# The gate matrix of a PEER layer from 2-byte one-hots made on VectorE, with the gate in three 2-byte parts

## The chip, the core and the metric

The kernel runs on one core of a Trainium2 chip. The metric is the device time in microseconds (us) of one execution. Before the change it is 2056.32 us, the median of three runs (2055.21 to 2059.06).

## The reference, cut to what matters

One layer of a diffusion backbone: a token-mixing part (differential attention, a spatial gating branch, gated merge) and then a channel-mixing part, PEER: 512 tokens, 8 heads, and for each token and head the best 16 of 128 x 128 = 16384 single-neuron experts.

```python
s1, i1 = lax.top_k(s[:, :, 0], 16)       # per token and head, 128 keys on each side
s2, i2 = lax.top_k(s[:, :, 1], 16)
cand = s1[..., :, None] + s2[..., None, :]          # 256 candidates
best, pos = lax.top_k(cand, 16)
eidx = (i1 * 128 + i2) picked by pos                # expert number
gate = softmax(best)
act = gelu(x . u_tab[eidx]) * gate                  # per token, head, pick
out = sum over picks of act * v_tab[eidx]
```

So each token has 128 picks (8 heads x 16), each with a first key number, a second key number and a gate in 4-byte floats.

## The kernel before, in words

The layer runs as one hand-ordered program. The engines POOL, VectorE (DVE), ScalarE (ACT) and TensorE (PE) execute their instructions in the order in which the code emits them (`manual_schedule`, `by_hand`, L218 and L692). The token-mixing part comes first and is not touched.

PEER is done in two ways. One block of 128 tokens (block 3) gathers its picks row by row with indirect DMAs on POOL (`fetch`, `dot`, `accumulate`, L805 to L823, stepped by `gather_to`, L836). The other three blocks (NB = 3, 384 tokens) are computed densely against all 16384 experts, 128 experts at a time: `u_pass(b)` (L773) makes GELU(u . x) for 128 experts and 384 tokens on PE with 24 matmuls, writes it through the SP queue to HBM for the first 74 passes, and `v_pass(b)` (L1156) later multiplies by the gate matrix G and by the second table. Each pass takes its weights from a loader (`w_get`, L192): a DMA on the SP queue, `w_hi` on ACT (L170), `w_lo` on DVE (L181), three passes ahead with three buffers each.

G is what the change is about. For one token, G is a 128 x 128 matrix: entry (first key, second key) is the gate of that pick. The kernel makes it as a matrix product over the 128 picks: a one-hot of the second key of every pick (`oa`, picks on the partitions, 128 keys along the free dimension) times a one-hot of the first key scaled with the gate (`ob`). The stage has 48 batches (t, o) of 8 tokens each.

- `picks_of(t)` (L1035): three PE transposes of a block's key numbers and gates, and one ACT copy to `pk`.
- `one_hots_a` (L1049): ACT, eight Square activations of 128 elements (iota minus key, squared) and one Relu of 1024 elements (1 minus it) per batch.
- `one_hots_b` (L1058): DVE, eight TENSOR_SCALAR of 128 elements per batch (equal to the key, times the gate).
- `gate_matrix` (L1067): PE, eight 4-byte matmuls of 128 x 128 x 128 per batch (the profile has two records for each), two ACT copies out of PSUM into `stg`, and after each second batch one DMA of 1 MB to HBM (`G_d`, L1081).

The loop (L1095 to L1106) emits for batch i: one-hots b of batch i+1, the gate matmuls of batch i, one `u_pass`, one-hots a of batch i+2, some 2.8 us of the top-16 and merge work of later blocks on DVE (`advance`, L946, until that is used up), the second half of a gather step that is pending (`gather_end`, L825), and from batch 10 to 42 new gather steps: a dot on DVE, a fetch on POOL. A gather step's GELU (L818) is on ACT, between a dot and an `acc` on DVE. After the loop come the last u passes, and then the v passes, of which the first needs a load of G back from HBM (`Gc`, L1142).

Of the kernel before, what the change touches and what calls it, by code (L numbers as in the profile page):

```python
# [13 lines left out]
F32 = mybir.dt.float32  # L14
F32R = mybir.dt.float32r
BF16 = mybir.dt.bfloat16
I32 = mybir.dt.int32
U32 = mybir.dt.uint32
AF = mybir.ActivationFunctionType
ALU = mybir.AluOpType  # L20
# [4 lines left out]
P = 128  # L25
# [33 lines left out]
def body(ctx, nc, tc, a, out):  # L59
# [11 lines left out]
    ones = cp.tile([P, P], F32, name="ones")  # L71
# [284 lines left out]
    with att, tc.tile_pool(name="at1", bufs=1) as a1, tc.tile_pool(name="at2", bufs=2) as a2, \  # L356
# [6 lines left out]
        for k in range(2):  # L363
            nc.vector.scalar_tensor_tensor(ld, lamr[:, k * 128:k * 128 + 64], 1.0, lamr[:, k * 128 + 64:k * 128 + 128],
                                           op0=ALU.mult, op1=ALU.mult, accum_out=le[:, k:k + 1])
# [171 lines left out]
    with tc.tile_pool(name="sg1", bufs=1) as s1, tc.tile_pool(name="sg2", bufs=2) as s2:  # L537
# [6 lines left out]
        with tc.tile_pool(name="pz", bufs=1, space=PSUM) as pzp, tc.tile_pool(name="pu", bufs=2, space=PSUM) as pu:  # L544
# [10 lines left out]
            for half in range(2):  # L555
                pz = [pzp.tile([P, 512], F32, name=f"pz{t}") for t in range(NT)]
                for c2 in range(4):
# [6 lines left out]
                    for cc in range(2):  # L564
                        c = c2 * 2 + cc
                        r = slice(cc * 512, cc * 512 + 512)
                        for t in range(NT):
                            q = slice(t * P, t * P + P)
# [82 lines left out]
            for j in range(NH):  # L651
                po = pu.tile([P, T], F32, name="ps_ot", tag="ps_m")
                for t in range(NT):
# [3 lines left out]
                                               op0=ALU.mult, op1=ALU.subtract)  # L657
# [3 lines left out]
            for i, n in enumerate(LAST):  # L661
# [14 lines left out]
                                           op0=ALU.add, op1=ALU.mult)  # L676
# [16 lines left out]
    with tc.tile_pool(name="o1", bufs=1) as o1, tc.tile_pool(name="o2", bufs=2) as o2:  # L693
        rowt = {}
        for i, k in enumerate(("gg1", "sh2", "gsc2")):
            t = o1.tile([P, D], F32, name=f"row_{k}")
# [128 lines left out]
    def gather_end(left=0):  # L825
        while len(pend) > left:
            accumulate(*pend.pop(0))
# [8 lines left out]
    def gather_to(share):  # L836
        while steps and n_steps - len(steps) < n_steps * share:
            gather_step()

    gS = {}  # L840
    with tc.tile_pool(name="k1", bufs=1, side="right") as k1:
        iota_i = k1.tile([P, P], I32, name="iota_i")
        nc.gpsimd.iota(iota_i, pattern=[[1, P]], base=0, channel_multiplier=0)
        iota = k1.tile([P, P], F32, name="iota")
# [88 lines left out]
        def next_u():  # L933
            if nu[0] < n_ahead:
                gS[nu[0]] = u_pass(nu[0])
                nu[0] += 1
# [9 lines left out]
        def advance(us):  # L946

            while us > 0 and any(todo):
                q = todo[0] or todo[1]
                d = next(q[0], None)  # L950
                if d is None:
                    q.popleft()
                else:
                    us -= d
            return any(todo)
# [73 lines left out]

        with tc.tile_pool(name="pg", bufs=3, space=PSUM) as pgp, tc.tile_pool(name="k2", bufs=2, side="right") as k2:  # L1030
            stg = {}

            pks, oas, obs = {}, {}, {}

            def picks_of(t):  # L1035

                while t not in pks:
                    while t not in done:
                        advance(1.0)
                    ef = efs.pop(t)  # L1040
                    pt = pgp.tile([P, 3, P], F32, name="ps_pk", bufs=1)
                    for k in range(2):
                        nc.tensor.transpose(pt[:, k], ef[:, k].rearrange("p h k -> p (h k)"), ident)
                    nc.tensor.transpose(pt[:, 2], gate[:, t], ident)
                    pks[t] = k2.tile([P, 3, P], F32, name="pk")
                    nc.scalar.activation(pks[t], pt, AF.Copy)
                return pks[t]

            def one_hots_a(t, o):  # L1049

                pk = picks_of(t)
                oa = oas[t, o] = k2.tile([P, 8, P], F32, name="oh_a", bufs=3)
                for i in range(8):
                    k = o * 8 + i
                    nc.scalar.activation(oa[:, i], iota, AF.Square, scale=-1.0, bias=pk[:, 1, k:k + 1])  # L1055
                nc.scalar.activation(oa, oa, AF.Relu, scale=-1.0, bias=ones[:, 0:1])

            def one_hots_b(t, o):  # L1058

                t0 = o * 8  # L1060
                pk = picks_of(t)
                ob = obs[t, o] = k2.tile([P, 8, P], F32, name="oh_b")
                for i in range(8):
                    nc.vector.tensor_scalar(ob[:, i], iota, pk[:, 0, t0 + i:t0 + i + 1], pk[:, 2, t0 + i:t0 + i + 1],  # L1064
                                            op0=ALU.is_equal, op1=ALU.mult)

            def gate_matrix(t, o):  # L1067

                oa, ob = oas.pop((t, o)), obs.pop((t, o))
                if o % 2 == 0:  # L1070
                    stg[0] = k2.tile([P, NBLK // GCH, 16, GCH], F32, name="stg")
                for q in range(2):
                    pG = pgp.tile([P, 4, P], F32, name="ps_G")
                    for i in range(4):
                        nc.tensor.matmul(pG[:, i], oa[:, q * 4 + i], ob[:, q * 4 + i], start=True, stop=True)  # L1075
                    tt = o % 2 * 8 + q * 4
                    nc.scalar.activation(stg[0][:, :, tt:tt + 4].rearrange("p c t g -> p t c g"),
                                         pG.rearrange("p t (c g) -> p t c g", g=GCH), AF.Copy)
                if o % 2:
                    tt = t * P + o // 2 * 16  # L1080
                    nc.sync.dma_start(G_d[:, :, tt:tt + 16].rearrange("c p t g -> p c (t g)"),  # L1081
                                      stg[0].rearrange("p c t g -> p c (t g)"))

            batches = [(t, o) for t in range(NB) for o in range(16)]
            while 0 not in done:
                advance(4.0)
                next_u()
            for _ in range(UA):
                next_u()
            one_hots_a(*batches[0])  # L1090
            for _ in range(UB):
                next_u()
            one_hots_a(*batches[1])
            one_hots_b(*batches[0])
            for i, (t, o) in enumerate(batches):  # L1095
                if i + 1 < len(batches):
                    one_hots_b(*batches[i + 1])
                gate_matrix(t, o)
                if nu[0] < n_ahead - RESERVE:
                    next_u()  # L1100
                if i + 2 < len(batches):
                    one_hots_a(*batches[i + 2])
                advance(2.8)
                gather_end()
                if i >= G_FROM:
                    gather_to(PICKS_G * (i + 1 - G_FROM) / (G_TO - G_FROM) if i < G_TO else 0)  # L1106
            advance(1000.0)
            while nu[0] < n_ahead:
                next_u()
# [181 lines left out]
```

## Time and profile before

| | before |
|---|---|
| median of 3 runs, us | 2056.32 |
| the profiled execution, us | 2059.31 |
| its span (first to last instruction), us | 2057.1 |
| mean granted TensorE clock | 0.984 |
| stage of the gate matrix: first gate matmul to the start of the last batch's, us in the span | 955.1 to 1271.5 |

The profiled execution's own time is 3 us above the median; differences are worked out against it and then put onto the median. "Idle before, releaser" in a row is the time that the engine stood still before the instruction and what ended that. In a timeline row, "xN" means N instructions of the same kind one after the other, and the duration is that of all of them. PEld is the weight load of a matmul, which overlaps with PE. A wait for several things is put down to the one that came last.

### The profile page before, as it was taken

How to read it: one execution, taken by the hardware profiler on the slowest of the kernel's cores; microseconds unless marked ns; L12 is line 12 of the kernel's file. 1: busy time of each engine (PE TensorE's matmuls, PEld its weight loads, DVE VectorE, ACT ScalarE, POOL GpSimd, SP SyncE). 2: the span in 40 equal slices, each digit the busy share in tenths (PEclk: the TensorE clock that was granted, in tenths of full speed). 3: DMA queues.
4: the chain of work that ended last, by engine and by line, in shares of the span. 5: the costliest groups of instructions: out<-in, count | busy, mean ns of one | idle time of the engine just before them, and what ended most of it. 6: DMA issues, size and time to landing. Idle time of an engine off the chain costs nothing.

```text
span 2057.1 us, 28286 instructions
## 1 busy us (share of the span) xinstructions
PE 1928.1 (94%) x10042; PEld 1693.9 (82%) x10042; DVE 1609.0 (78%) x3070; ACT 1016.5 (49%) x1963; POOL 451.5 (22%) x275
## 2 busy tenths in 40 slices
PE   5699999999999899889899999899999999999997
PEld 3478888887888788688888999688888889999996
DVE  6957777736766657999998785688888789899987
ACT  4345555544333355446989987333333333333333
POOL 4832232101000124330002110011111233333321
PEclk9899999999999999999999999999999999999999
DMA  7452323344867355346659999899998789989982
GB/s 240 162 158 71 98 72 98 88 159 136 263 210 239 123 163 162 117 160 214 188 183 318 309 316 295 306 322 334 324 334 317 270 340 353 342 326 344 348 313 98
DMA packets 167772, 473.91 MB, mean 230 GB/s; under 512 B 14000, under 2 KB 82512, under 8 KB 149072
## 3 DMA queue, kind: packets, MB, share of 16 engines
q1 hardware_dynamic: 149200, 337.89, 49.4%
q0 software_dynamic: 18432, 134.23, 17.8%
q8 instruction: 79, 1.29, 0.2%
q14 instruction: 61, 0.50, 0.1%
HBM read 415.29 MB, written 48.38 MB: 225 GB/s over the span
## 4 chain that ended last, share of the span: by engine, by line
PE 63%; DVE 19%; issue 7%; DMA 5%; ACT 4%; POOL 1%; SPq 0%; ACTq 0%; DVEq 0%; POOLq 0%
PE po L200 8%; PE po L201 8%; PE po L199 8%; PE ps_u L201 5%; PE ps_u L200 5%; PE ps_u L199 5%; DVE w_lo L181 3%; PE ps_G L1075 2%; PE ps_proj L199 2%; PE ps_proj L200 2%; PE ps_proj L201 2%; DVE ada_j L274 2%; PE ps_s L455 2%; DMA ada_w<-in_wada 2%; ACT oh_a L1055 1%
## 5 line engine op out<-in xcount | busy, mean ns | idle before, releaser
L170 ACT ACTIVATE w_hi<-w_raw 128x1024 fp32r<-128x1024 f32 x370 | 390.8, 1057 | 458.5 <-issue 280.2
L181 DVE TENSOR_TENSOR w_lo<-w_raw,w_hi 128x1024 fp32r<-128x1024 f32 x324 | 397.9, 1229 | 170.7 <-ACT w_hi L170 170.1
L807 POOL DMA_INDIRECT uv<-in_uv,eidx x128 | 207.5, 1621 | 876.1 <-DVE acc L823 536.8
L201 PE MATMUL ps_u<-h2B,w_lo 128*128 128x384 f32 x1024 | 348.3, 340 | 16.4 <-DVE w_lo L181 16.4
L199 PE MATMUL ps_u<-h2B,w_hi 128*128 128x384 f32 x1024 | 352.3, 344 | 1.1 <-ACT h2B L739 1.1
L200 PE MATMUL ps_u<-h2B,w_hi 128*128 128x384 f32 x1024 | 347.0, 339 | 0.6 <-DVE r L84 0.6
L199 PE MATMUL po<-w_hi,ah 128*128 128x512 f32 x768 | 303.8, 396 | 7.5 <-ACT ah L1148 7.5
L200 PE MATMUL po<-w_lo,ah 128*128 128x512 f32 x768 | 303.7, 396 | 0.2 <-DVE w_lo L181 0.2
L201 PE MATMUL po<-w_hi,al 128*128 128x512 f32 x768 | 303.8, 396 | 0.0
L201 PEld LDWEIGHTS ps_u<-h2B,w_lo 128*128 128x128 f32 x1024 | 194.2, 190 | 19.3 <-DVE w_lo L181 19.3
L199 PEld LDWEIGHTS ps_u<-h2B,w_hi 128*128 128x128 f32 x1024 | 194.9, 190 | 4.1 <-ACT h2B L739 1.4
L200 PEld LDWEIGHTS ps_u<-h2B,w_hi 128*128 128x128 f32 x1024 | 194.6, 190 | 3.8 <-DVE r L84 1.0
L199 PEld LDWEIGHTS po<-w_hi,ah 128*128 128x128 f32 x768 | 144.4, 188 | 40.4 <-ACT ah L1148 7.8
L201 PEld LDWEIGHTS po<-w_hi,al 128*128 128x128 f32 x768 | 144.2, 188 | 35.0
L200 PEld LDWEIGHTS po<-w_lo,ah 128*128 128x128 f32 x768 | 144.3, 188 | 33.9 <-DVE w_lo L181 1.0
L823 DVE SCALAR_TENSOR_TENSOR acc<-uv,act,acc 128x1024 f32<-128x1024 f32 x127 | 163.2, 1285 | 4.5
L814 DVE SCALAR_TENSOR_TENSOR dj<-uv,h2A 128x1024 bf16<-128x1024 f32 x128 | 156.2, 1220 | 0.9
L181 POOL TENSOR_TENSOR w_lo<-w_raw,w_hi 128x1024 fp32r<-128x1024 f32 x46 | 114.7, 2497 | 180.0 <-ACT w_hi L170 179.9
L1146 DVE TENSOR_TENSOR at<-gS,Gc 128x384 f32<-128x384 f32 x128 | 120.9, 945 | 8.1 <-DMA gS<-gS_d 8.1
L1148 ACT ACTIVATE ah<-at 128x384 fp32r<-128x384 f32 x128 | 65.9, 515 | 123.6 <-DVE at L1146 123.5
L781 ACT ACTIVATE gS<-ps_u 128x384 f32<-128x384 f32 x128 | 62.7, 490 | 127.9 <-PE ps_u L201 127.3
L1075 PE MATMUL ps_G<-oh_b,oh_a 128*128 128x128 f32 x768 | 100.8, 284 | 24.8 <-DVE oh_b L1064 24.3
(302 smaller groups left out, 3562.6 us busy)
## 6 DMA issues: line engine op xcount, KB each, us to landing
w_raw<-in_uT SPq DMA_DIRECT2D x128, 512.0 KB, 5.8
w_raw<-in_uv SPq DMA_DIRECT2D x128, 512.0 KB, 6.6
w_raw<-in_w SPq DMA_DIRECT2D x120, 512.0 KB, 3.6
G_d<-stg SPq DMA_DIRECT2D x24, 1024.0 KB, 6.0
Gc<-G_d SPq DMA_DIRECT2D x16, 1536.0 KB, 9.9
w_raw<-in_wada SPq DMA_DIRECT2D x32, 512.0 KB, 4.4
gS_d<-gS SPq DMA_DIRECT2D x74, 192.0 KB, 4.0
gS<-gS_d SPq DMA_DIRECT2D x74, 192.0 KB, 4.6
```

Of the source, the lines that this page charges most:

```text
L170: nc.scalar.activation(hi, r, AF.Copy)
L181: eng.tensor_tensor(lo, r, hi.bitcast(F32), op=ALU.subtract)
L199: nc.tensor.matmul(ps, lh, rh, start=first, stop=False)
L200: nc.tensor.matmul(ps, lh, rl, start=False, stop=False)
L201: nc.tensor.matmul(ps, ll, rh, start=False, stop=last)
L781: nc.scalar.activation(g, ps, AF.Gelu)
L807: nc.gpsimd.indirect_dma_start(out=g, out_offset=None, in_=a["uv"], in_offset=bass.IndirectOffsetOnAxis(ap=eidx[:, t - NB, k:k + 1], axis=0))
L814: nc.vector.scalar_tensor_tensor(junk, g[:, :D], 1.0, h2A[t - NB], op0=ALU.mult, op1=ALU.mult, accum_out=act)
L823: nc.vector.scalar_tensor_tensor(acc[t - NB], g[:, D:], act, acc[t - NB], op0=ALU.mult, op1=ALU.add)
L1075: nc.tensor.matmul(pG[:, i], oa[:, q * 4 + i], ob[:, q * 4 + i], start=True, stop=True)
L1146: nc.vector.tensor_tensor(at, gS.pop(b), Gc[b // GCH][:, :, b % GCH], op=ALU.mult)
L1148: nc.scalar.activation(ah, at, AF.Copy)
```

## The change

The one-hots become 2-byte floats (key numbers up to 127 are exact in them), made for eight tokens by one DVE instruction each; ACT makes none any more. A gate of 24 bits is split into three 2-byte parts whose sum is the gate, so `ob` has three tiles, and the gate matmul of one token becomes three matmuls that add up in PSUM. Per batch DVE gets five TENSOR_TENSOR of 1024 elements (`oa`, `eq`, three products) in place of eight TENSOR_SCALAR of 128 elements; ACT loses eight Square and one Relu; PE has 24 matmuls of 2-byte data in place of 16 records of 4-byte data. The per-token operand is stored twice side by side ([P, 5, P, 2]) so that its innermost dimension is a run of two elements. `picks_of` gets two more ACT copies and two DVE subtractions. `oa` has two buffers and not three, and it is made one batch ahead and not two.

```diff
@@ -1029,7 +1029,9 @@
 
         with tc.tile_pool(name="pg", bufs=3, space=PSUM) as pgp, tc.tile_pool(name="k2", bufs=2, side="right") as k2:
             stg = {}
-
+            PAIR = [P, 8, P // 2, 2]
+            iota2 = k2.tile([P, P // 2, 2], BF16, name="iota2", bufs=1)
+            nc.vector.tensor_copy(iota2, iota.rearrange("p (a b) -> p a b", b=2))
             pks, oas, obs = {}, {}, {}
 
             def picks_of(t):
@@ -1042,27 +1044,37 @@
                     for k in range(2):
                         nc.tensor.transpose(pt[:, k], ef[:, k].rearrange("p h k -> p (h k)"), ident)
                     nc.tensor.transpose(pt[:, 2], gate[:, t], ident)
-                    pks[t] = k2.tile([P, 3, P], F32, name="pk")
-                    nc.scalar.activation(pks[t], pt, AF.Copy)
+                    pk = pks[t] = k2.tile([P, 5, P, 2], BF16, name="pk")
+                    nc.scalar.activation(pk[:, 0:3], pt.unsqueeze(3).to_broadcast([P, 3, P, 2]), AF.Copy)
+                    rest_ = k2.tile([P, P], F32, name="g_rest", bufs=1)
+                    nc.vector.tensor_tensor(rest_, pt[:, 2], pk[:, 2, :, 0], op=ALU.subtract)
+                    for k in range(3, 5):
+                        nc.scalar.activation(pk[:, k], rest_.unsqueeze(2).to_broadcast([P, P, 2]), AF.Copy)
+                        if k == 3:
+                            nc.vector.tensor_tensor(rest_, rest_, pk[:, k, :, 0], op=ALU.subtract)
                 return pks[t]
 
+            def per_token(pk, k, o):
+                return pk[:, k, o * 8:o * 8 + 8].unsqueeze(2).to_broadcast(PAIR)
+
+            def pairs(x):
+                return x.rearrange("p t (a b) -> p t a b", b=2)
+
             def one_hots_a(t, o):
 
+                oa = oas[t, o] = k2.tile([P, 8, P], BF16, name="oh_a")
+                nc.vector.tensor_tensor(pairs(oa), iota2.unsqueeze(1).to_broadcast(PAIR), per_token(picks_of(t), 1, o),
+                                        op=ALU.is_equal)
+
+            def one_hots_b(t, o):
+
                 pk = picks_of(t)
-                oa = oas[t, o] = k2.tile([P, 8, P], F32, name="oh_a", bufs=3)
-                for i in range(8):
-                    k = o * 8 + i
-                    nc.scalar.activation(oa[:, i], iota, AF.Square, scale=-1.0, bias=pk[:, 1, k:k + 1])
-                nc.scalar.activation(oa, oa, AF.Relu, scale=-1.0, bias=ones[:, 0:1])
-
-            def one_hots_b(t, o):
-
-                t0 = o * 8
-                pk = picks_of(t)
-                ob = obs[t, o] = k2.tile([P, 8, P], F32, name="oh_b")
-                for i in range(8):
-                    nc.vector.tensor_scalar(ob[:, i], iota, pk[:, 0, t0 + i:t0 + i + 1], pk[:, 2, t0 + i:t0 + i + 1],
-                                            op0=ALU.is_equal, op1=ALU.mult)
+                eq = k2.tile([P, 8, P], BF16, name="oh_e", bufs=1)
+                nc.vector.tensor_tensor(pairs(eq), iota2.unsqueeze(1).to_broadcast(PAIR), per_token(pk, 0, o),
+                                        op=ALU.is_equal)
+                ob = obs[t, o] = k2.tile([P, 3, 8, P], BF16, name="oh_b")
+                for k in range(3):
+                    nc.vector.tensor_tensor(pairs(ob[:, k]), pairs(eq), per_token(pk, 2 + k, o), op=ALU.mult)
 
             def gate_matrix(t, o):
 
@@ -1072,7 +1084,8 @@
                 for q in range(2):
                     pG = pgp.tile([P, 4, P], F32, name="ps_G")
                     for i in range(4):
-                        nc.tensor.matmul(pG[:, i], oa[:, q * 4 + i], ob[:, q * 4 + i], start=True, stop=True)
+                        for k in range(3):
+                            nc.tensor.matmul(pG[:, i], oa[:, q * 4 + i], ob[:, k, q * 4 + i], start=k == 0, stop=k == 2)
                     tt = o % 2 * 8 + q * 4
                     nc.scalar.activation(stg[0][:, :, tt:tt + 4].rearrange("p c t g -> p t c g"),
                                          pG.rearrange("p t (c g) -> p t c g", g=GCH), AF.Copy)
@@ -1088,18 +1101,16 @@
             for _ in range(UA):
                 next_u()
             one_hots_a(*batches[0])
+            one_hots_b(*batches[0])
             for _ in range(UB):
                 next_u()
-            one_hots_a(*batches[1])
-            one_hots_b(*batches[0])
             for i, (t, o) in enumerate(batches):
                 if i + 1 < len(batches):
+                    one_hots_a(*batches[i + 1])
                     one_hots_b(*batches[i + 1])
                 gate_matrix(t, o)
                 if nu[0] < n_ahead - RESERVE:
                     next_u()
-                if i + 2 < len(batches):
-                    one_hots_a(*batches[i + 2])
                 advance(2.8)
                 gather_end()
                 if i >= G_FROM:
```

## Rows read from the trace of the kernel before

**Rows 1.** The page's part 1: engine, busy us, share of the span, instructions

```profile
PE 1928.1 (94%) x10042; PEld 1693.9 (82%) x10042; DVE 1609.0 (78%) x3070; ACT 1016.5 (49%) x1963; POOL 451.5 (22%) x275
```

**Rows 2.** Windows A, B, C: us, busy PE, PEld, DVE, ACT, POOL; PEclk, DMA share, GB/s

```profile
955.14:1067.76 112.62, 102.38 (x643) 98.69 (x644) 108.86 (x331) 99.81 (x214) 0.13 (x1) 0.98 0.57 174
1067.76:1253.60 185.84, 172.19 (x1124) 168.71 (x1124) 148.42 (x347) 166.79 (x387) 33.23 (x23) 1.00 0.94 310
1253.60:1271.50 17.90, 17.90 (x121) 17.90 (x121) 10.04 (x29) 17.53 (x39) 0.00 (x0) 1.00 0.91 285
```

**Rows 3.** Timeline of stretch A, one batch (start us, us, instruction): DVE, then PE

```profile
1044.02 2.14 DVE L1064 TENSOR_SCALAR oh_b<-iota,pk 128x128 f32<-128x128 f32 x8
1046.06 1.22 DVE L181 TENSOR_TENSOR w_lo<-w_raw,w_hi 128x1024 fp32r<-128x1024 f32 x1
1047.20 1.22 DVE L912 TENSOR_TENSOR eq<-ij,iota 128x1024 f32<-128x1024 f32 x1
1048.45 1.22 DVE L916 TENSOR_TENSOR eq<-eq,idxf 128x1024 f32<-128x1024 f32 x1
...
1050.85 2.13 DVE L1064 TENSOR_SCALAR oh_b<-iota,pk 128x128 f32<-128x128 f32 x8
...
1051.34 2.19 PE L1075 MATMUL ps_G<-oh_b,oh_a 128*128 128x128 f32 x16 [0.46 <-DVE oh_b L1064]
```

**Rows 4.** Timeline of stretch B, one batch: ACT, DVE, PE

```profile
1120.95 0.49 ACT L781 ACTIVATE gS<-ps_u 128x384 f32<-128x384 f32 x1 [1.59 <-PE ps_u L201]
1121.34 2.44 ACT L1055 ACTIVATE oh_a<-iota,pk 128x128 f32<-128x128 f32 x8
...
1124.87 0.18 ACT L818 ACTIVATE act<-act 128x1 f32<-128x1 f32 x1
...
1125.09 0.16 DVE L819 TENSOR_TENSOR act<-act,gate 128x1 f32<-128x1 f32 x1 [1.80 <-ACT act L818]
...
1128.12 2.19 PE L1075 MATMUL ps_G<-oh_b,oh_a 128*128 128x128 f32 x16 [1.24 <-DVE oh_b L1064]
```

**Rows 5.** Timeline of stretch C: two gate groups on PE

```profile
1259.57 1.95 PE L1075 MATMUL ps_G<-oh_b,oh_a 128*128 128x128 f32 x16
...
1265.53 1.95 PE L1075 MATMUL ps_G<-oh_b,oh_a 128*128 128x128 f32 x16
```

**Rows 6.** Timeline behind the stage: SP, then PE

```profile
1274.11 0.37 SPq L1081 DMA_DIRECT2D G_d<-stg  x1
...
1293.48 0.79 PE L199 MATMUL po<-w_hi,ah 128*128 128x512 f32 x1 [7.53 <-ACT ah L1148]
```

**Rows 7.** Groups by form, 955 to 1275 us: count, busy us, mean ns, idle before

```profile
L912 DVE TENSOR_TENSOR eq<-ij,iota 128x1024 f32<-128x1024 f32 x8 | 9.8, 1219 | 0.0
...
L821 DVE TENSOR_SCALAR acc<-uv,act 128x1024 f32<-128x1024 f32 x1 | 0.8, 752 | 0.0
L877 DVE TENSOR_TENSOR cand<-val 128x512 f32<-128x512 f32 x1 | 0.7, 693 | 0.0
...
L923 DVE TENSOR_TENSOR gate<-gate,gz 128x128 f32<-128x128 f32 x2 | 0.6, 292 | 0.1
```

**Rows 8.** Timeline of PE: first and last of 7 starts with 384 columns, of 6 with 512

```profile
1262.06 0.34 PE L200 MATMUL ps_u<-h2B,w_hi 128*128 128x384 f32 x1
...
1263.10 0.34 PE L200 MATMUL ps_u<-h2B,w_hi 128*128 128x384 f32 x1
...
1399.85 0.40 PE L199 MATMUL po<-w_hi,ah 128*128 128x512 f32 x1
...
1401.01 0.39 PE L201 MATMUL po<-w_hi,al 128*128 128x512 f32 x1
```

**Rows 9.** Timeline of the stage's first us: ACT, then DVE

```profile
948.38 0.48 ACT L1046 ACTIVATE pk<-ps_pk 128x384 f32<-128x384 f32 x1
...
953.51 1.23 DVE L181 TENSOR_TENSOR w_lo<-w_raw,w_hi 128x1024 fp32r<-128x1024 f32 x1 [2.26 <-ACT w_hi L170]
...
960.27 1.23 DVE L181 TENSOR_TENSOR w_lo<-w_raw,w_hi 128x1024 fp32r<-128x1024 f32 x1 [1.42 <-ACT w_hi L170]
```

## The prediction

> **What bounds the kernel now.** I read the page's part 1 first: PE is busy for 94% of the span, ACT for 49% [rows 1]. That mean says nothing of the stage that is edited, so I cut the stage into three stretches by the starts of the gate groups [rows 2]. A holds batches 0 to 15 (16 in 112.62 us, 7.04 a batch), B batches 16 to 43 (28 in 185.84, 6.64 a batch), C batches 44 to 46 (5.97 a batch). In A the DVE is busy 108.86 of 112.62 us: it is full, with the top-16 and merge work of later blocks beside the one-hots. In B it is busy 148.42 of 185.84 (5.30 a batch), PE 172.19. In C PE has no gap at all.
>
> One batch of A [rows 3]: oh_b starts at 1044.02, w_lo and merge work follow back to back, the next oh_b starts at 1050.85. The gate group on PE starts at 1051.34, after 0.46 us of idle ended by DVE's oh_b, and takes 2.19 us because it follows oh_b token by token. So A goes at DVE's pace, and ACT's speed is of no use there. One batch of B [rows 4]: ACT finishes a u pass with gS at 1120.95, and only after eight Squares and a Relu comes the small act of a gather step, at 1124.87. DVE has waited 1.80 us for it, runs the acc and dot behind it, then oh_b, and PE's next gate group starts 1.24 us late. In B the work that leaves ACT does stand on the path, in some batches. In C PE's own period shows: 1259.57 to 1265.53 is 5.96 us, one gate group and one u pass [rows 5]. Behind the stage the last gate group sets the end: its G goes to HBM at 1274.11, and PE stands 7.53 us idle until the first v pass starts at 1293.48 [rows 6]. The u passes that are left finish inside that gap, so a shift of the last gate group moves the end by as much.
>
> **What DVE loses and gets.** Out go eight TENSOR_SCALARs a batch: 1046.06 - 1044.02 = 2.04 us of DVE [rows 3]. In come five TENSOR_TENSORs of 1,024 2-byte elements. No row shows a TENSOR_TENSOR with all operands of two bytes. From above: 4-byte ones of this size take 1.219 us [rows 7], start to start 1.14 where independent and 1.25 where one reads the other's result [rows 3]. From below: a 128-element oh_b starts every 0.255 us (2.04 / 8), and no DVE instruction with eight times the elements should go under that. Between them, the one-source TENSOR_SCALAR of 1,024 elements takes 0.752, and the 512-element TENSOR_TENSOR 0.693 [rows 7]; 1.219 against 0.693 gives 1.03 ns an element. I take two 2-byte elements in the time of one 4-byte element, the price of the 512-element row: 0.693 - 0.08 (the overlap in 1.22 to 1.14) = 0.61 independent, and 0.72 for the one that waits for eq. A batch is 4 x 0.61 + 0.72 = 3.16, so +1.12 on DVE.
>
> The Trainium skill (Vector Engine (DVE) Microarchitecture Reference, section 5.1) says two-source ops take two 2-byte elements a cycle when every operand's innermost step is one and longer than one element; the doubled operand meets that, and by it the price is mine. Its section 5.2 speaks against: a port that does not read adjacent pairs of 4-byte words from an 8-byte boundary loses about 0.65 cycle an element; worked out from its figures this is an estimate of some 1.0 us an instruction.
>
> A row bears on that: L912 reads one operand's element 16 times in a row and still takes 1.219, like w_lo with dense operands [rows 3, 7]. A repeated read cost nothing there, so the sum keeps 0.61.
>
> **Stretch A and the start.** The one-hots of batches 0 to 16 are made up to A's end: 17 x 1.12 = 19.0 us on a full DVE. Against that, two waits of DVE for w_hi at the start, 2.26 and 1.42 us [rows 9], stand behind the Squares and Relus on ACT and go. Net +15. Cover lost: PE's gate group can no longer follow oh_b token by token, as its first matmul needs the third product. That costs nothing while DVE sets the pace: gate group plus u pass is under 6 us against 8 on DVE.
>
> **The picks, three times.** ACT's pk copy takes 0.48 for 384 elements [rows 9]; with each element stored twice I put 0.8. Then DVE subtracts (0.29, the 128-element row [rows 7]), ACT copies (0.3 to 0.5), DVE subtracts, ACT copies. DVE stands in order: behind the first subtraction wait the one-hots, w_lo and the merge. Some 1 us a block, since oa and eq cover the last copy: +3. On PE the transposes keep their place; the block-1 dot now lies ahead of the subtraction and covers the pk copy. The cast of iota is one 0.3 us instruction. SP's and POOL's queues keep their order.
>
> **PE.** Six starts of 384 columns take 1.04 us, 0.173 each [rows 8]; a u pass has 24, 4.15. The period of 5.96 [rows 5] leaves 1.81 to the gate group's 16 starts, 0.113 each. The new group has 24 starts. Lower end: five starts of 512 columns take 1.16, 0.232 each [rows 8], so 128 columns are 0.059 and 128 columns alone 0.173 - 2 x 0.059 = 0.055; with a little on top I write 0.066, a group of 1.6 and a period of 5.75. Upper end: 0.113 again, a group of 2.7 and a period of 6.87. The 128-column row is slower than its columns, and what is left to explain that is the weight load. With 2-byte weights half as many bytes are loaded, so I take a value under 0.098, where PE (4.15 plus 24 starts) stays under DVE's period in B. The upper end stays for the range and as a rival.
>
> **Stretch B.** DVE's work is 5.30 + 1.12 = 6.42 a batch. The waits for act go: with no Square and Relu between gS and act, act comes about 3.5 us earlier (1121.34 to 1124.87 [rows 4]). 23 of the 28 batches have a gather step (POOL's count [rows 2]); without one DVE works 10.04 / 3 = 3.35 a batch as in C [rows 2], 4.5 after the change, with one some 6.8. The short batches cannot use all they gain, since the next acc still waits for the u pass. I put 6.46 in place of 6.64: 28 x 0.18 = -5. What is late next is DVE itself. The transfers stand near: share 0.94 at 6.64 [rows 2], so no period under 6.64 x 0.94 = 6.24.
>
> **Stretch C.** PE sets the pace: 3 x (5.97 - 5.75) plus the last group, -1.
>
> **Sum:** +15 + 3 - 5 - 1 = +12. The profiled execution, 2059.3, is 3 us over the median; on the median, 2056.3 + 12 = 2068.
>
> **The rivals.**
> 1. *DVE at the full price.* Each TENSOR_TENSOR costs as a 4-byte one: 4 x 1.14 + 1.25 = 5.8 a batch, +3.8. A gets 17 x 3.8 - 4 = +61, B goes to 9.1, 28 x 2.5 = +69, C +3, picks +3: +136, 2192. The 752 ns row shows a DVE that can do better with one source [rows 7], none shows it with two. 0.09.
> 2. *The repeated word is read at less than full pace.* The per-token operand reads the same four bytes 64 times in a row, in all five instructions. Halfway between 0.61 and 1.14, 0.87, a batch is 4 x 0.87 + 0.99 = 4.5, +2.4: A 17 x 2.4 - 4 = +37, B 28 x (7.7 - 6.64) = +30, picks +3: +70, 2126. L912 speaks against it [rows 7]. 0.04. This is the case of the skill's section 5.2, above.
> 3. *PE becomes the bound in B and C.* At 0.113 a start B goes to 6.87, 28 x 0.23 = +6, and C with the last group gets +4: +15 + 3 + 6 + 4 = +28, 2084. For it: the same 128-column shape. Against: half the bytes. 0.20.
> 4. *The other side: the one-hots cost DVE no more than now, and the ACT waits of B go.* Place: the five instructions. It decides where A's loss equals B's gain, which the transfers cap at 28 x 0.40 = 11: 17 x (added) - 4 + 3 - 1 = 11 gives 0.76 added a batch, 0.54 an instruction; under about 0.48 the kernel is faster by over 0.2%. At 0.40 it is 17 x 0.08 - 4 + 3 - 11 - 1 = -12, 2044. Against: 0.54 is no more than 512 elements at the 1.03 ns of the rows. 0.05.
> 5. *B fills up fully.* My price holds, but B reaches its 6.24 and the start hides a little more: +13 + 3 - 11 - 1 = +4, 2060. 0.09.
>
> **How the numbers follow.** My forecast has 0.53. A measurement of this kernel can tell about 0.2%, 4 us, from no change. Slower: forecast, rivals 1 to 3, 0.85; within 0.2%: most of rival 5 and a little of the forecast's spread, 0.10; faster 0.05. The range takes in rivals 5 and 3 with the spread of the picks (2 below the one, 4 above the other), 2058 to 2088; it leaves out rivals 1, 2 and 4, 0.18.
>
> **What would show it.** Right: in A a period near 8 us with DVE without gaps and PE idle about 2 us a batch ahead of the gate group, ended by DVE's ob; 0.69 for a TENSOR_TENSOR; in B ACT idle, no wait of DVE for act over 1 us, periods of 6.3 to 6.6; gate starts under 0.098. Wrong: DVE instructions at 1.2; PE without a gap in B; a granted clock that drops in A, where PE stands longer (it is 0.98 there now [rows 2]), enough that the u passes outlast DVE's 8 us; or gaps on DVE in A that I took for work.

## The result, and the profile after

The changed kernel takes 2068.64 us (median of 5 runs, 2067.29 to 2069.57), the kernel before 2056.87 in the same comparison: a ratio of 1.0054, 95% interval 1.0041 to 1.0067. That is 11.8 us slower; +12 and 2068 were forecast. The number is right, but not every term of it: a wait that was left out (+4.3) and a gain that was put too small (by 4.6) cancel, as the stretches and run 1 show. That the total came out so near is luck in part.

The same three stretches as in [rows 2], cut at the starts of the same gate groups (us, busy PE, PEld, DVE, ACT, POOL; granted clock, DMA share, GB/s), of the changed kernel:

```profile
957.54:1087.99 130.45, 105.85 (x773) 97.77 (x771) 127.07 (x286) 48.67 (x74) 0.94 (x1) 0.92 0.49 149
1087.99:1265.23 177.24, 164.16 (x1347) 153.86 (x1348) 175.00 (x260) 77.33 (x138) 33.73 (x22) 1.00 0.99 327
1265.23:1282.05 16.82, 16.82 (x145) 16.31 (x145) 14.17 (x20) 7.91 (x12) 0.00 (x0) 1.00 1.00 323
```

A went from 112.62 to 130.45 us (+17.8), B from 185.84 to 177.24 (-8.6), C from 17.90 to 16.82 (-1.1). DVE is now full in A and in B (127.07 of 130.45, 175.00 of 177.24), ACT is busy for less than half of either. The stage begins 2.4 us later in its span (957.54 against 955.14), although this execution was 1.0 us ahead shortly before (run 1 has the rows).

The groups by form of the changed kernel over the stage: count, busy us, mean ns, idle before (`oh_e` is the name of the tile `eq`):

```profile
L1077 DVE TENSOR_TENSOR oh_b<-oh_e,pk 128x1024 bf16<-128x1024 bf16 x144 | 90.9, 686 | 1.7
L1088 PE MATMUL ps_G<-oh_b,oh_a 128*128 128x128 bf16 x1145 | 85.5, 223 | 37.7 <-DVE oh_b L1077 37.7
L1088 PEld LDWEIGHTS <-oh_a 128*128 128x128 bf16 x1146 | 69.0, 99 | 56.7 <-issue 32.7 <-DVE oh_b L1077 23.2 <-DVE w_lo L181 0.3
...
L1073 DVE TENSOR_TENSOR oh_e<-iota,pk 128x1024 bf16<-128x1024 bf16 x47 | 32.1, 683 | 0.0
L1066 DVE TENSOR_TENSOR oh_a<-iota,pk 128x1024 bf16<-128x1024 bf16 x47 | 32.1, 683 | 0.0
```

A 1,024-element instruction on 2-byte operands takes 0.683 to 0.686 us, within 0.01 us of the 512-element 4-byte row [rows 7]. The timeline of one batch of A, DVE and then PE, of the changed kernel:

```profile
1058.45 0.68 DVE L1066 TENSOR_TENSOR oh_a<-iota,pk 128x1024 bf16<-128x1024 bf16 x1
1059.05 0.69 DVE L1073 TENSOR_TENSOR oh_e<-iota,pk 128x1024 bf16<-128x1024 bf16 x1
1059.77 1.89 DVE L1077 TENSOR_TENSOR oh_b<-oh_e,pk 128x1024 bf16<-128x1024 bf16 x3
...
1061.58 1.22 DVE L181 TENSOR_TENSOR w_lo<-w_raw,w_hi 128x1024 fp32r<-128x1024 f32 x1
```

```profile
1060.52 0.23 PE L1088 MATMUL ps_G<-oh_b,oh_a 128*128 128x128 bf16 x1 [1.10 <-DVE oh_b L1077]
1061.11 0.22 PE L1088 MATMUL ps_G<-oh_b,oh_a 128*128 128x128 bf16 x1 [0.37 <-DVE oh_b L1077]
1061.71 1.39 PE L1088 MATMUL ps_G<-oh_b,oh_a 128*128 128x128 bf16 x22 [0.38 <-DVE oh_b L1077]
1068.43 0.23 PE L1088 MATMUL ps_G<-oh_b,oh_a 128*128 128x128 bf16 x1 [1.10 <-DVE oh_b L1077]
```

From oh_a to the w_lo behind the products is 3.13 us (1058.45 to 1061.58), where oh_b took 2.04 [rows 3]. This batch lasts 7.91 us (1060.52 to 1068.43) against 6.83 in the same place before. PE waits 1.10 us ahead of the group and twice 0.4 inside it, once for each further product.

What the prediction had at almost nothing is the cast of iota (DVE, changed kernel):

```profile
919.08 0.23 DVE L1034 CAST iota<-iota 128x128 bf16<-128x128 f32 x1 [4.35 <-PE ps_sc L984]
```

The matmuls that end this wait, on PE:

```profile
917.99 1.05 PE L984 MATMUL ps_sc<-keysT,qT 128*128 128x128 f32 x8
```

DVE stands still for 4.35 us. The tile for the 2-byte iota is taken from a pool that opens where the query stage's pool closes, so its memory is that of tiles of which the last is read by the score matmuls L984; those stand behind a u pass on PE.

In B no wait for act is left: over all of B DVE waited 26.7 us for it before the change, in 11 waits, and not once after. The timeline of one batch of B in the changed kernel, ACT and then DVE (compare [rows 4]):

```profile
1107.44 0.19 ACT L818 ACTIVATE act<-act 128x1 f32<-128x1 f32 x1
...
1108.07 1.22 DVE L181 TENSOR_TENSOR w_lo<-w_raw,w_hi 128x1024 fp32r<-128x1024 f32 x1
...
1109.20 0.15 DVE L819 TENSOR_TENSOR act<-act,gate 128x1 f32<-128x1 f32 x1
1109.39 1.28 DVE L823 SCALAR_TENSOR_TENSOR acc<-uv,act,acc 128x1024 f32<-128x1024 f32 x1
```

The act is done 1.6 us before DVE comes to it. Behind the stage nothing changed: from the start of the last gate group to the end of the span it is 785.8 us, 785.6 before, and PE stands there as in [rows 6]:

```profile
1303.62 0.79 PE L199 MATMUL po<-w_hi,ah 128*128 128x512 f32 x1 [7.51 <-ACT ah L1159]
```

### The profile page after: what moved, and what is told of

Read it like the earlier page. It is cut to its first block, busy times and chain, and to the rows that moved or that the text cites. A ratio compares the mean times of both kernels' runs of the same rounds, so it can differ in the third digit from the quotient of the medians.

```text
span 2067.8 us, 28429 instructions
## 1 busy us (share of the span) xinstructions
PE 1926.7 (93%) x10426; PEld 1680.6 (81%) x10426; DVE 1657.6 (80%) x2933; ACT 863.6 (42%) x1537; POOL 457.5 (22%) x275
## 3 DMA queue, kind: packets, MB, share of 16 engines
q0 software_dynamic: 18432, 134.23, 17.6%
## 4 chain that ended last, share of the span: by engine, by line
PE 62%; DVE 25%; issue 7%; DMA 3%; ACT 2%; POOL 1%; SPq 0%; POOLq 0%; DVEq 0%; ACTq 0%
PE po L199 8%; PE po L201 8%; PE po L200 8%; PE ps_u L201 5%; PE ps_u L199 5%; PE ps_u L200 5%; DVE w_lo L181 4%; DVE oh_b L1077 3%; PE ps_proj L199 2%; PE ps_proj L200 2%; PE ps_proj L201 2%; DVE ada_j L274 2%; PE ps_s L455 2%; PE ps_o L489 1%; DMA w_raw<-in_wada 1%
## 5 line engine op out<-in xcount | busy, mean ns | idle before, releaser
L807 POOL DMA_INDIRECT uv<-in_uv,eidx x128 | 212.6, 1661 | 882.7 <-DVE acc L823 551.7
L199 PE MATMUL ps_u<-h2B,w_hi 128*128 128x384 f32 x1024 | 356.7, 348 | 1.1 <-ACT h2B L739 1.1
L200 PE MATMUL ps_u<-h2B,w_hi 128*128 128x384 f32 x1024 | 350.8, 343 | 0.6 <-DVE r L84 0.6
L199 PEld LDWEIGHTS ps_u<-h2B,w_hi 128*128 128x128 f32 x1024 | 197.9, 193 | 4.3 <-ACT h2B L739 1.5
L200 PEld LDWEIGHTS ps_u<-h2B,w_hi 128*128 128x128 f32 x1024 | 197.8, 193 | 3.8 <-DVE r L84 1.0
L814 DVE SCALAR_TENSOR_TENSOR dj<-uv,h2A 128x1024 bf16<-128x1024 f32 x128 | 156.1, 1219 | 0.9
L1088 PE MATMUL ps_G<-oh_b,oh_a 128*128 128x128 bf16 x1152 | 85.9, 223 | 37.7 <-DVE oh_b L1077 37.7
```

The source lines that it names most:

```text
L199: nc.tensor.matmul(ps, lh, rh, start=first, stop=False)
L200: nc.tensor.matmul(ps, lh, rl, start=False, stop=False)
L807: nc.gpsimd.indirect_dma_start(out=g, out_offset=None, in_=a["uv"], in_offset=bass.IndirectOffsetOnAxis(ap=eidx[:, t - NB, k:k + 1], axis=0))
L814: nc.vector.scalar_tensor_tensor(junk, g[:, :D], 1.0, h2A[t - NB], op0=ALU.mult, op1=ALU.mult, accum_out=act)
L1088: nc.tensor.matmul(pG[:, i], oa[:, q * 4 + i], ob[:, k, q * 4 + i], start=k == 0, stop=k == 2)
```

## The experiments

Theory: in A and in B VectorE sets the pace, so a batch's cost is what its one-hots cost DVE; the gain in B is that act no longer stands behind one-hot work on ACT; the cast's wait adds 4 us. Rivals: the 24 matmuls set the pace, or the gain in B comes from ACT's smaller load or the shorter gate groups. Rows of windows below have the columns of [rows 2].

**1. The 2-byte iota made early (iota_early).**

```diff
-            iota2 = k2.tile([P, P // 2, 2], BF16, name="iota2", bufs=1)
+        iota2 = k1.tile([P, P // 2, 2], BF16, name="iota2")   # and its cast, at the start of the PEER part
```

> The changed kernel with the 2-byte iota made at the start of the PEER part, in a buffer of its own, and not in the pool whose memory the query stage held until then. Theory: the cast's wait of 4.35 us on VectorE lies on the full engine ahead of stretch A, so nearly all of it comes back: about 2064.5 us, 4 us under the changed kernel, the three stretches as they were (130, 177, 17 us). Rival: the 3.3 us by which the stage began late in the changed kernel are drift between two executions, or VectorE makes up for them elsewhere: 2068.6 us.

2063.99 us (ratio to before 1.0031, 1.0020 to 1.0043), 4.65 under the changed kernel between the medians. The first gate group starts at 954.60, A and B stay:

```profile
954.60:1085.10 130.50, 106.45 (x772) 98.43 (x770) 127.11 (x286) 48.97 (x74) 0.94 (x1) 0.91 0.49 149
1085.10:1262.44 177.34, 164.22 (x1347) 153.84 (x1348) 175.10 (x260) 77.35 (x138) 33.69 (x22) 1.00 0.98 326
```

The starts of two executions cannot be compared as they stand, since they had drifted apart before the cast. The same w_lo ahead of the cast's place, in before, the changed kernel and this run:

```profile
912.18 3.51 DVE L181 TENSOR_TENSOR w_lo<-w_raw,w_hi 128x1024 fp32r<-128x1024 f32 x3
```

```profile
911.22 3.50 DVE L181 TENSOR_TENSOR w_lo<-w_raw,w_hi 128x1024 fp32r<-128x1024 f32 x3
```

```profile
912.57 3.51 DVE L181 TENSOR_TENSOR w_lo<-w_raw,w_hi 128x1024 fp32r<-128x1024 f32 x3
```

From there to the first gate group it is 42.96 us before, 46.32 in the changed kernel and 42.03 here. So 4.3 us of the wait and the cast (4.35 and 0.23) reached the stage, and behind it nothing made up for them. One instruction of 0.23 us, placed where its buffer was not free, was more than a third of the slowdown.

**2. One product, three matmuls of it (one_product).**

```diff
-                for k in range(3):
+                for k in range(1):
                     nc.vector.tensor_tensor(pairs(ob[:, k]), pairs(eq), per_token(pk, 2 + k, o), op=ALU.mult)
...
-nc.tensor.matmul(pG[:, i], oa[:, q * 4 + i], ob[:, k, q * 4 + i], start=k == 0, stop=k == 2)
+nc.tensor.matmul(pG[:, i], oa[:, q * 4 + i], ob[:, 0, q * 4 + i], start=k == 0, stop=k == 2)
```

> The changed kernel with one product per batch in place of three, and three matmuls that all read it: left out are the second and third part of the gate (the first is added three times). VectorE has 2 x 0.60 us less per batch, TensorE the same work. Theory (VectorE sets the pace of A and B): A 130.5 - 16 x 1.2 = 111 us, B down to TensorE's period or the transfers' share, 28 x 5.6 to 6.2 = 157 to 174 us, total 2040 to 2050. Rival (the 24 matmuls set the pace): nothing changes, 2068.

2027.69 us (one execution). Windows A and B:

```profile
955.19:1066.64 111.45, 93.46 (x772) 88.76 (x771) 107.91 (x253) 49.02 (x74) 0.94 (x1) 0.98 0.56 174
1066.64:1223.22 156.58, 156.58 (x1348) 152.25 (x1348) 142.90 (x204) 77.37 (x138) 33.68 (x22) 1.00 1.04 368
```

A lost 19.0 us, 1.19 a batch, the price of two products. B fell from 177.24 to 156.58, 5.59 us a batch over its 28, which is PE's own pace without a gap (156.58 busy of 156.58). The total is below the expected one: that reckoned with a B held up by its transfers, at up to 174 us. No such floor shows: the share reads 1.04 at 368 GB/s.

**3. Three products, one matmul (one_matmul).**

```diff
-                        for k in range(3):
-                            nc.tensor.matmul(pG[:, i], oa[:, q * 4 + i], ob[:, k, q * 4 + i], start=k == 0, stop=k == 2)
+                        nc.tensor.matmul(pG[:, i], oa[:, q * 4 + i], ob[:, 2, q * 4 + i], start=True, stop=True)
```

> The changed kernel with all three products made but one matmul per token, of the last part: left out of the sum are the first two parts of the gate. TensorE has 16 x 0.056 = 0.9 us less per batch, VectorE the same work. Theory (VectorE sets the pace of A and B): A and B within 1 us of 130.5 and 177, C 3 x 0.9 = 3 us shorter, total about 2065. Rival (TensorE sets the pace): A and B lose 0.9 us a batch, 40 us in all, 2028.

2066.91 us (one execution). Windows A and B:

```profile
958.23:1088.73 130.50, 92.61 (x515) 87.84 (x515) 127.12 (x286) 47.48 (x74) 0.93 (x1) 0.87 0.48 151
1088.73:1266.33 177.60, 146.42 (x899) 138.37 (x899) 174.80 (x259) 72.91 (x136) 33.67 (x22) 0.93 0.98 326
```

With two thirds of the gate matmuls gone, A and B are the same to 0.4 us, and PE only idles more. C, where PE is full, loses 2.8 us (14.06 between the same starts). The rival of the 24 matmuls is out.

**4. The kernel before with ScalarE's one-hots emitted later (before_oa_late).**

```diff
-                if i + 2 < len(batches):
-                    one_hots_a(*batches[i + 2])
                 advance(2.8)
                 gather_end()
+                if i + 2 < len(batches):
+                    one_hots_a(*batches[i + 2])
```

> The kernel before with one edit: the eight Squares and the Relu of a batch are emitted behind the gather step's act and acc, and not ahead of them. No one-hot changes its engine. Theory (the gain in B came from act no longer standing behind 3.5 us of one-hot work on ScalarE): A stays at 112.6 us, B falls from 185.8 to 28 x 6.0 to 6.3 = 168 to 176, total about 2045. Rival (the gain in B came from ScalarE having less to do, or from the shorter gate matmuls): B stays near 185, total 2057.

2042.16 us, a ratio of 0.9915 (0.9901 to 0.9928): two lines moved, no instruction changed. ACT's timeline, then windows A and B:

```profile
1122.05 0.49 ACT L781 ACTIVATE gS<-ps_u 128x384 f32<-128x384 f32 x1
...
1122.43 0.19 ACT L818 ACTIVATE act<-act 128x1 f32<-128x1 f32 x1
1122.53 2.44 ACT L1055 ACTIVATE oh_a<-iota,pk 128x128 f32<-128x128 f32 x8
```

```profile
955.20:1067.87 112.67, 102.42 (x644) 98.78 (x644) 108.90 (x332) 99.79 (x214) 0.20 (x1) 0.98 0.57 174
1067.87:1235.55 167.68, 167.68 (x1125) 167.47 (x1125) 148.61 (x347) 166.06 (x387) 33.17 (x23) 1.00 1.00 344
```

act now comes right behind gS and the Squares behind act. A is as it was, B falls to 167.68 (5.99 a batch, PE full, ACT busy 166.06). ACT's load and the matmuls are unchanged, so neither was what cost time in B; the order was. The change made this gain as well, and gave more than half of it back to DVE.

**5. The third product on POOL (third_on_pool).**

```diff
-                    nc.vector.tensor_tensor(pairs(ob[:, k]), pairs(eq), per_token(pk, 2 + k, o), op=ALU.mult)
+                    (nc.gpsimd if k == 2 else nc.vector).tensor_tensor(pairs(ob[:, k]), ...)   # on top of 1
```

> The kernel with the early iota, and the third of the three products made by POOL instead of VectorE. Theory (VectorE sets the pace of A and B): 0.61 us less per batch on VectorE, A 130.5 - 16 x 0.61 = 120.7 us, B from 177 to 28 x 5.7 to 5.9 = 160 to 165 us, total about 2040. Rival (POOL's product comes later than the engine that it relieves, or the two engines get in each other's way at their memory): TensorE waits for POOL, VectorE's rows grow over 0.69, and the total stays at 2060 or above.

2120.39 us, 1.0306 (1.0289 to 1.0322): a miss, and the rival's sign. A took 148.10, B 210.12. DVE and POOL in one batch:

```profile
1105.03 0.68 DVE L1073 TENSOR_TENSOR oh_e<-iota,pk 128x1024 bf16<-128x1024 bf16 x1
1105.74 2.99 DVE L1077 TENSOR_TENSOR oh_b<-oh_e,pk 128x1024 bf16<-128x1024 bf16 x2
1105.85 2.33 POOL L1077 TENSOR_TENSOR oh_b<-oh_e,pk 128x1024 bf16<-128x1024 bf16 x1 [2.78 <-DVE oh_e L1073]
```

Two products took 2.99 us in place of 1.3: while POOL's product runs (2.33 us), one of DVE's two does not get on (its longest took 2.39 us, its shortest 0.69). The Trainium skill (SBUF — State Buffer, "Who interferes with whom") says that VectorE and GpSimd share a pair of memory ports as an exclusive lock, and that a VectorE instruction with two inputs in SBUF contends with a GpSimd instruction that reads SBUF. The run agrees: the product that POOL took would have cost DVE 0.61 us, and the two left to DVE took 1.7 us longer (2.99 against 1.3). The difference is what A lost against run 1: 17.6 us over 16 batches, 1.1 each.

**6. Three engines (three_engines).** As 5, and for batches 0 to 15 the second key's one-hot by ACT, 2-byte, emitted behind act.

```diff
+                    nc.scalar.activation(oa[:, i], iota, AF.Square, scale=-1.0, bias=k2nd[0][:, k:k + 1])   # batches 0 to 15
+                nc.scalar.activation(oa, oa, AF.Relu, scale=-1.0, bias=ones[:, 0:1])
```

> As the one with the third product on POOL, and for the first 16 batches the one-hot of the second key is made by ScalarE again (eight Squares and a Relu with a 2-byte result, emitted behind the gather's act). Theory: in A VectorE has one comparison and two products, 1.94 us against 2.04 before, so A is 111 to 113 us; B as with the third product on POOL, 160 to 165; total 2030 to 2035, under both kernels and under the kernel before with the late Squares (2042). Rival (ScalarE's one-hots hold up the other work on ScalarE in A): A stays over 118 and nothing is won over the third product on POOL alone.

2115.94 us, 1.0282 (1.0263 to 1.0300): a miss too. A 139.84 (148.10 in run 5), B 210.31: A shortens by 8.3 us, near what one comparison less on DVE should bring (16 x 0.6 = 9.6; where the rest went was not traced), but POOL's product spoils both.

**7. The per-token operand with an innermost step of 0 (single).**

```diff
-                return pk[:, k, o * 8:o * 8 + 8].unsqueeze(2).to_broadcast(PAIR)
+                return pk[:, k, o * 8:o * 8 + 8, 0].unsqueeze(2).to_broadcast([P, 8, P])   # the other views lose their pairs too
```

> The changed kernel with the per-token operand read with an innermost step of 0 (one element 128 times) in place of a stored pair read 64 times. Same instructions, same counts, same result. Theory (two elements at a time need two neighbours in every operand): each of the five instructions goes from 0.684 to about 1.22 us, 2.7 us more per batch, A 130 + 16 x 2.7 = 173, B 28 x 9.0 = 252, total about 2185. Rival (2-byte elements alone give the pace): 0.684 stays, 2068.

2196.47 us (one execution). The instructions that write ob (ns, shortest, median, longest), and windows A and B:

```profile
L1077 DVE TENSOR_TENSOR oh_b<-oh_e,pk x144: 1215/1219/1228, 959.7 to 1406.9; 128x1024 bf16<-128x1024 bf16 x144
```

```profile
960.97:1134.13 173.16, 119.44 (x771) 110.65 (x770) 169.79 (x286) 49.28 (x74) 0.94 (x1) 0.82 0.37 114
1134.13:1386.10 251.97, 196.47 (x1347) 182.53 (x1347) 249.75 (x259) 76.55 (x136) 36.89 (x22) 0.87 0.72 231
```

Two bytes alone bring nothing: with a per-token operand that has no neighbour to read, each of these instructions takes 1.219 us, exactly as with 4-byte operands. The pair layout is worth 128 us here, and rival 1's 2192 was the time without it.

**8. Two parts, no POOL (two_parts_mixed).** As 6 with all products on DVE, and two of them.

```diff
-                for k in range(3):
-                    (nc.gpsimd if k == 2 else nc.vector).tensor_tensor(pairs(ob[:, k]), ...)
+                for k in range(2):
+                    nc.vector.tensor_tensor(pairs(ob[:, k]), ...)   # and two matmuls per token
```

> No work on POOL; the gate in two 2-byte parts and not three, so the last 8 of its 24 bits are left out; for the first 16 batches the one-hot of the second key on ScalarE (2-byte result, emitted behind the gather's act), for the other 32 on VectorE. Theory (each stretch goes at the pace of the engine that is full there): A has 0.60 x 2 + 0.72 = 1.9 us on VectorE in place of 2.04, 111 us; B has 5.30 - 2.04 + 4 x 0.61 + 0.1 = 5.8 at most, 28 x 5.6 to 5.8 = 157 to 162; C 3 x (4.15 + 16 x 0.056) = 15; total 2025 to 2032, under the kernel before with the late Squares (2042). Rival (VectorE's 2-byte instructions hold up other engines too, as POOL's did): B over 168, no gain over 2042.

2033.33 us, 0.9880 (0.9862 to 0.9898), 1 us over the expected range; it keeps 16 of the gate's 24 bits. Only run 2, which leaves out more, is faster. B is as expected:

```profile
951.89:1067.24 115.35, 93.95 (x643) 89.00 (x644) 107.89 (x253) 97.39 (x209) 1.34 (x1) 0.93 0.55 165
1067.24:1228.64 161.40, 149.45 (x1123) 140.53 (x1123) 157.65 (x231) 73.36 (x137) 33.69 (x22) 1.00 1.03 360
```

A is 4 us over the 111 expected: DVE is busy for only 107.89 of 115.35 us. Its w_lo waits 5.7 us in A for w_hi, with one-hots on ACT again. With the whole gate, the fastest is run 4.

## Why the prediction was right, and where its terms were not

- **What bounds the stretches: right.** Runs 2 and 3 separate DVE from PE in A and B, and C moves with PE alone.
- **DVE's price: right.** 0.61 and 0.72 were taken; the starts in A are 0.60 and 0.72 apart, a batch 3.13 against 3.16. Run 7 shows what decides it: the broadcast operand needs two neighbours as well. That agrees with the rule that the prediction takes from the Trainium skill (Vector Engine (DVE) Microarchitecture Reference, section 5.1), with 1219 and 684 ns beside it. The loss that I drew from section 5.2 of that page of the Trainium skill for a repeated word did not appear: 684 ns an instruction, against the estimate of some 1.0 us.
- **A and the start: right.** +15, and two of the three picks, were +17. In run 1, which has no wait for iota, A grew by 17.9 and its start, counted from the w_lo, came 0.9 us earlier: +17.0. The picks' wait inside, 0.5 us for ACT between the subtractions, is there.
- **The cast of iota: wrong.** "One 0.3 us instruction" cost 4.3 us (run 1; 4.65 between the medians). I priced the instruction and not the memory under its tile. The trace of before had the L984 matmuls and their place on PE, and the diff shows the tile in the new pool; both would have given the wait.
- **B: mis-sized.** The forecast was 6.46 us a batch, 6.42 of DVE's work and 0.04 that the short batches cannot use; it was 177.24 / 28 = 6.33. DVE is idle 2.2 us in all of B, 0.08 a batch, so it is the work that was put too high: 175.00 / 28 = 6.25. The +1.12 a batch came from rows of A; in B DVE's busy time grew by 26.6 us, 0.95 a batch. A part of that is that the stretch before held 231 of the TENSOR_SCALARs that go, where 28 batches have 224; the rest was not traced. The mechanism, no wait for act, was right (run 4). -5, and +1 for the third pick, were -8.6.
- **The transfers' floor of 6.24: wrong.** B ran at 5.59 a batch in run 2. A share of 0.94 did not say how near a limit was.
- **PE: right, at the lower end.** 22 starts of the group take 1.39 us with the last one's 0.22 in it, so 0.056 each; 0.066 was written, and under 0.098 PE was to stay below DVE's period in B. C's period is 5.58 (1270.89 to 1276.47).

```profile
1270.89 1.51 PE L1088 MATMUL ps_G<-oh_b,oh_a 128*128 128x128 bf16 x24
1276.47 1.51 PE L1088 MATMUL ps_G<-oh_b,oh_a 128*128 128x128 bf16 x24
```

- **Cover lost: harmless, but told wrongly.** The group's first matmul waits for the first product, not the third; the second and third matmul wait 0.4 us each for theirs.

The measured sum is +17.0 (start and A) + 4.3 (cast) - 8.6 (B) - 1.1 (C) = +11.6, against +11.8 between the medians. Without the cast's wait the kernel is at 2064 (run 1), inside the range that was forecast but 4 us under its point. A right total is no proof of the terms.

## What to carry to other kernels

Before work is moved off an engine, look which engine is full in each stretch: here the work went to the engine that was full, and the gain of the move (an act that no longer stood in line) was to be had by emitting the same work two lines later on the engine where it was. A tile in a pool that has just opened can have to wait for the last reader of whatever lay there (4.35 us here): an instruction with no cost of its own belongs where its buffer has long been free. With 2-byte operands a two-source VectorE instruction of this size took 684 ns in place of 1219 only when the broadcast operand, too, had two neighbours in its innermost dimension.

## What was not expected of the hardware

- POOL's 2.33 us TENSOR_TENSOR holds up a TENSOR_TENSOR on DVE until it is over (run 5). An idle POOL is not a free place for DVE's work.
- In A, where PE now stands longer, its granted clock fell: 0.92 against 0.98 before, 0.87 in run 3, 0.82 in run 7. In one batch, after PE stood 1.61 us, the 22 matmuls took 2.19 us in place of 1.39: the first started every 0.055 us, the later ones every 0.107, at a granted clock of 0.50 (989 to 990 us), the lower of the two levels, 1.2 GHz. It cost the end nothing, as DVE was full: A took 130.50 us at 0.91 (run 1) and at 0.87 (run 3). The changed kernel's rows:

```profile
986.84 0.23 PE L1088 MATMUL ps_G<-oh_b,oh_a 128*128 128x128 bf16 x1 [1.61 <-DVE oh_b L1077]
...
988.04 2.19 PE L1088 MATMUL ps_G<-oh_b,oh_a 128*128 128x128 bf16 x22 [0.38 <-DVE oh_b L1077]
```

- A gate group on 2-byte weights starts a matmul every 0.056 us, where with 4-byte ones each of a matmul's two records took 0.113: the weight load's record falls from 0.19 to 0.099 us.
